# The last group's output products by half, and the third group's output projection at the end of the list

## The chip, the cores and the metric

The kernel runs on one core of a Trainium2 chip. The metric is the device time of one launch in microseconds (us). The five engines of the core have their own instruction streams: TensorE (PE, with its weight loads PEld), VectorE (DVE), ScalarE (ACT), GpSimd (POOL) and SyncE (SP), which issues most of the DMA. They wait for each other by semaphores only.

## The reference

One inference step of a trunk with two layers. 128 prompt tokens and 512 sample tokens, 640 in all, each a row of D = 1024 numbers in f32. Each layer is

```
h = rms_norm(x, g) * (1 + scale) + shift        # scale, shift, gate from SiLU(cond)
x = x + gate * branch(h)
```

Layer 0's branch is a Conformer convolution. Layer 1's branch, the one that the change touches, is a Mamba-2 scan in both directions:

```
u = h @ w_in                                    # z, x, b, c and the time steps
x, b, c = silu(depthwise_conv(x b c))           # 5 taps
y = scan forwards + scan backwards + d_skip * x # chunks of 128 tokens, 4 groups of 512 channels
y = rms_norm per group(y * silu(z)) @ w_out
```

Each scan works by chunks: within a chunk a 128x128 product of c and b, masked by decays, times x; between chunks a state that is carried on. A last RMSNorm of x with its gain gives the two outputs y; the scan's final states are outputs too.

## The kernel before

All matrix products are made in three: a number is split into a rounded part (hi) and the rest (lo), and a product is hi·hi + lo·hi + hi·lo. So 12 products of 128x512 stand for one output half chunk (128 tokens, 512 of the 1024 columns): four pieces of the 512 channels of a group, three products each.

Layer 1 is cut in tiles. The list `PLAN1` gives their order: `x`, `b`, `c`, `z` with a group and a number are projections of h (each 48 products of 128x320, line L1301), and `o` with a group and a half is the output projection of a finished group for one half of the columns (`out2`, 5 chunks of 12 products of 128x512, L1552). The generator `filler` takes them one by one. Group 3's output projection is not in the list: `last_products` makes it (L1907), chunk by chunk in the order `LAST` (4, 3, 0, 2, 1).

Beside the tiles runs the scan of each group (`group`): pcb (c times b, L1743), pst (a chunk's state, L1632), py (the masked product times x, L1763), po (the state's part, L1695) and pty (a transpose, L1722) on TensorE. On DVE stand the mask and decays (gf, L1571 and L1754), the state (stn, L1660), the state's part of y (yo, L1699), the transposed sum (xt, L1726), the multiplication by silu(z) (zs, L1781), the squares for the group's norm (ysq, L1827 and L1828), and the split of y in hi and lo (yl, L1810 or L1807). TensorE sums the squares (ssp, L1833). A drained product is scaled and gated by DVE (tmp, L1527, for the last group L1918) and added to x (L1531, L1921) by DVE or POOL. The convolution of the projections is on DVE too (L1345).

Nothing sets the order by hand. Each of these parts is a generator that yields operations with a guessed duration, keys it waits for and slots of rings of buffers it needs; the class `Order` keeps a clock for each engine and issues, again and again, the operation that can start first, with `PRIO1` deciding between equals. `run.lead` is the time that TensorE's operations are planned later than their inputs; it is 0.2 · (`PRIO1["lead"]` + 7), and 0.3 once `last_products` is through. So a new table gives another order of the same instructions. The real times are not those that the planner guessed: an engine works its list in order and waits where an input is late.

The last group's out weights, `w_out2[3, n]` for n = 0 to 3 (n = 0, 1 for half 0 of the columns, 2, 3 for half 1), come in four loads of 512 KB. Three go through the weight chain `w_chain` (buffers wf, wh, wl, DVE L1261), one is loaded late by `out_weights` into buffers that h leaves free after the last z tile (ACT L1874, DVE L1875). `last_products` waits for all four.

When both halves of a chunk have been added to x, with the sum of squares taken by ACT (L1922) as each half is done, DVE and ACT make the root of the mean square (`final`, L1929 to L1931), and `final_half` scales x (half 0 on ACT, L1945, after POOL has multiplied the gain, L1938; half 1 on DVE, L1947) and stores it (L1949).

## Time and profile before

| | us |
|---|---|
| median of 3 runs | 1062.21 (1061.73 to 1062.59) |
| profiled execution | 1061.69 |
| its span | 1059.8 |
| outside the span | 1.9 |
| PE busy | 1031.0 (97%) |
| DVE busy | 827.0 (78%) |
| ACT busy | 667.0 (63%) |
| POOL busy | 440.0 (42%) |
| first product of z32 | at 962.2 |
| end of z33, the last tile of the list | at 1002.5 |
| last product ends | at 1051.6 |

Times at the left of a row are microseconds from the start of the span. In rows of the timeline and of groups a line L12 is line 12 of the kernel, and `out<-in` names what is written and read. What stands in brackets at the end of a timeline row is how long the engine stood idle before it, and what ended that. A matmul on TensorE is pipelined: its length in a row is longer than the distance to the next one.

### The profile page before, as it was taken

How to read it: one execution, taken by the hardware profiler on the slowest of the kernel's cores; microseconds unless marked ns; L12 is line 12 of the kernel's file. 1: busy time of each engine (PE TensorE's matmuls, PEld its weight loads, DVE VectorE, ACT ScalarE, POOL GpSimd, SP SyncE). 2: the span in 40 equal slices, each digit the busy share in tenths (PEclk: the TensorE clock that was granted, in tenths of full speed). 3: DMA queues.
4: the chain of work that ended last, by engine and by line, in shares of the span. 5: the costliest groups of instructions: out<-in, count | busy, mean ns of one | idle time of the engine just before them, and what ended most of it. 6: DMA issues, size and time to landing. Idle time of an engine off the chain costs nothing.

```text
span 1059.8 us, 19157 instructions
## 1 busy us (share of the span) xinstructions
PE 1031.0 (97%) x7473; PEld 946.4 (89%) x7473; DVE 827.0 (78%) x1240; ACT 667.0 (63%) x1112; POOL 440.0 (42%) x443
## 2 busy tenths in 40 slices
PE   6999999999999999999999999999999999999986
PEld 3899999999999999999999988897879888998665
DVE  2599999998997689102678879789888687787897
ACT  6468788788687678433577666676556444572564
POOL 0029989978596511111000055335522544003642
PEclk9999999999999999999999999999999999999989
DMA  9598888788756667776212443434324344125413
GB/s 360 197 255 205 191 212 202 178 211 218 180 134 138 130 144 154 143 165 148 61 62 85 115 136 88 121 107 129 104 80 136 100 130 140 60 80 149 140 41 100
DMA packets 64362, 151.82 MB, mean 143 GB/s; under 512 B 9472, under 2 KB 22416, under 8 KB 64272
## 3 DMA queue, kind: packets, MB, share of 16 engines
q1 hardware_dynamic: 52480, 118.35, 36.0%
q0 software_dynamic: 8640, 30.94, 17.2%
q10 hardware_dynamic: 3152, 1.31, 0.5%
q8 instruction: 59, 0.97, 0.4%
q14 instruction: 31, 0.25, 0.1%
HBM read 145.45 MB, written 5.12 MB: 142 GB/s over the span
## 4 chain that ended last, share of the span: by engine, by line
PE 88%; DVE 5%; ACT 2%; DMA 2%; issue 2%; SPq 0%; POOL 0%; DVEq 0%; ACTq 0%; POOLq 0%
PE pz L1301 9%; PE xs L1301 8%; PE o L1552 8%; PE B L1301 2%; PE C L1301 2%; PE po L1695 2%; PE pst L1632 2%; PE o L1907 2%; PE py L1763 2%; PE o__4958 L157 1%; PE o__5267 L157 1%; PE o__5258 L157 1%; PE o__5245 L157 1%; PE o__4948 L157 1%; PE o__5238 L157 1%
## 5 line engine op out<-in xcount | busy, mean ns | idle before, releaser
L809 DVE SCALAR_TENSOR_TENSOR cva<-v,cst,cva 128x550 f32<-128x550 f32 (+12 forms) x346 | 270.2, 823 | 11.4 <-ACT cva L801 6.4
L881 POOL TENSOR_TENSOR cv<-cv,tp 128x490 f32<-128x490 f32 (+5 forms) x134 | 172.6, 1288 | 8.5
L840 ACT ACTIVATE tp<-v,cst 128x490 f32<-128x490 f32 (+5 forms) x134 | 92.4, 718 | 36.2 <-POOL cv L881 35.9
L424 ACT CAST wh<-wf 128x1024 fp32r<-128x1024 f32 x63 | 65.9, 1047 | 63.4 <-PE o__5267 L157 29.8
L1301 PE MATMUL pz<-h_hi,wh 128*128 128x320 f32 x256 | 86.3, 337 | 1.7 <-ACT up L1332 1.7
L1701 POOL TENSOR_TENSOR y<-y,yo 128x512 f32<-128x512 f32 x32 | 49.8, 1555 | 85.1 <-DVE yo L1699 81.5
L1301 PE MATMUL pz<-h_hi,wl 128*128 128x320 f32 x256 | 79.1, 309 | 0.0
L1301 PE MATMUL pz<-h_lo,wh 128*128 128x320 f32 x256 | 79.0, 309 | 0.0
L1301 PE MATMUL xs<-h_hi,wh 128*128 128x320 f32 x224 | 76.4, 341 | 0.0
L1345 DVE SCALAR_TENSOR_TENSOR xs<-up,cst,xs 128x642 f32<-128x642 f32 x64 | 66.3, 1037 | 10.2 <-ACT xs L1343 8.8
L1575 ACT ACTIVATE gf<-gf,cols 128x128 f32<-128x128 f32 x160 | 50.8, 391 | 29.8 <-DVE gf L1571 29.7
L1301 PE MATMUL xs<-h_hi,wl 128*128 128x320 f32 x224 | 69.3, 309 | 0.0
L1301 PE MATMUL xs<-h_lo,wh 128*128 128x320 f32 x224 | 69.1, 308 | 0.0
L1258 DVE TENSOR_TENSOR wl<-wf,wh 128x1024 fp32r<-128x1024 f32 x38 | 50.9, 1346 | 15.2 <-ACT wh L1249 15.2
L434 ACT ACTIVATE wl<-wh 128x1024 fp32r<-128x1024 f32 x58 | 61.6, 1061 | 1.7
L1569 POOL TENSOR_TENSOR gb<-gb,cols 128x512 f32<-128x512 f32 x20 | 25.1, 1255 | 85.6 <-DVE xs L1345 66.4
L435 POOL DMA_DIRECT2D wl<-w_in x43 | 37.4, 870 | 54.8 <-ACT wl L434 54.2
L1552 PE MATMUL o<-wh,yh 128*128 128x512 f32 x120 | 53.2, 443 | 0.0
L1301 PEld LDWEIGHTS pz<-h_hi,wh 128*128 128x128 f32 x256 | 48.1, 188 | 5.6 <-issue 3.4
L1249 ACT CAST wh<-wf 128x1024 fp32r<-128x1024 f32 x38 | 39.5, 1046 | 18.5 <-DMA wf<-w_xbc 6.1
L1301 PEld LDWEIGHTS pz<-h_lo,wh 128*128 128x128 f32 x256 | 48.2, 188 | 3.1 <-issue 2.9
L435 POOL DMA_DIRECT2D wl<-w_out x15 | 13.0, 865 | 90.4 <-ACT wl L434 90.4
(846 smaller groups left out, 3497.0 us busy)
## 6 DMA issues: line engine op xcount, KB each, us to landing
wf<-w_in SPq DMA_DIRECT2D x48, 512.0 KB, 3.7
wl<-w_in POOLq DMA_DIRECT2D x43, 512.0 KB, 6.6
wa<-w_ada SPq DMA_DIRECT2D x64, 256.0 KB, 5.8
wf<-w_out SPq DMA_DIRECT2D x32, 512.0 KB, 3.6
wf<-w_xbc SPq DMA_DIRECT2D x24, 512.0 KB, 3.6
gf<-acf SPq DMA_DIRECT2D x40, 256.0 KB, 4.2
wa<-w_ada SPq DMA_DIRECT2D x16, 512.0 KB, 10.6
wf<-w_z SPq DMA_DIRECT2D x16, 512.0 KB, 3.8
```

The costliest lines, as they stand in the source:

```text
L157: T.matmul(ps[:, b, at : at + t1 - t0], lhsT=w, rhs=h[:, t0:t1], start=first and n == 0, stop=last and n == 2)
L424: t = yield op(ACT, 1.05, lambda: S.copy(out=wh, in_=wf))
L434: yield op(ACT, 1.06, lambda: S.activation(out=wl, in_=wh.bitcast(F32), func=AF.Copy, scale=-1.0))
L435: t = yield op(PD, 0.7, lambda: G.dma_start(out=wl, in_=src, accum_op=ALU.add))
L809: t = yield op(VE, 0.24 + 0.01 * (hi - lo), lambda: V.scalar_tensor_tensor(out=rows64(accs[i], lo, hi), in0=rows64(vs[i], lo + d, hi + d), ...
L840: t = yield op(ACT, 0.72, lambda: S.activation(out=tp[:, :, 0 : hi - lo], in_=rows64(vs[i], lo + d, hi + d), func=AF.Copy, scale=w_dw(i, t ...
L881: t = yield op(PO, 1.3 + 0.019 * (hi - lo - 49), lambda: G.tensor_add(out=rows64(cv[i], lo, hi), in0=rows64(cv[i], lo, hi), in1=sgs["tp", ...
L1258: e_.tensor_sub(out=cell["wl"], in0=cell["wf"], in1=cell["wh"].bitcast(F32))
L1301: T.matmul(ps[:, b, at_ : at_ + t1 - t0], lhsT=w_, rhs=t_[:, t0:t1], start=k == 0 and n == 0, stop=k == nk - 1 and n == 2)
L1345: t = yield op(VL, 0.97, lambda: V.scalar_tensor_tensor(out=acc, in0=u[:, d : d + PW], scalar=c("w_c", j * 5 + d), in1=acc, op0=ALU.mult, ...
L1552: T.matmul(ps, lhsT=t_, rhs=w_, start=k == 0 and n == 0, stop=k == 3 and n == 2)
L1575: t = yield op(ACT, 0.39, lambda: S.activation(out=gv[:, h_, :], in_=gv[:, h_, :], func=AF.Exp, bias=cols1[ch][:, o8 + h_ : o8 + h_ + 1]), ...
```

## The change

There are four parts.

1. The tables `PRIO1`, `PLAN1` and `RB1` are others. In the list, z33 was the last tile, and half 1 of group 2's output projection (o21) stood ahead of it; now o21 is the last one, behind z33, and z30 and x32 have moved too. The planned lead of TensorE goes from 1.0 to 0.6. The ring xs gets 3 buffers instead of 2, st 6 instead of 7.
2. Of the last group's out weights two pieces come through the weight chain instead of three, and two are loaded late into the freed h buffers instead of one (`late_weights`, ACT L1878, DVE L1879). The late ones are those of half 1.
3. `last_products` is one generator for each chunk and half (L1910) and waits for the weights of its half only; halves of different chunks can change places. The lead of 0.3 is set when the first of them is through.
4. The last half chunk (chunk 1, half 1) is made in two pieces of 256 columns: 24 products of 128x256, two tmp (L1925), two additions to x (L1933), two squares (L1936), and one more addition of sums (L1946).

The diff, with its long tables cut:

```diff
-PRIO1 = {"lead": -2, ... "last_products": 3, "last_residual": 7, ... }
+PRIO1 = {"late_weights": -7, "lead": -4, ... "last_products": 5, "last_residual": -2, ... }
...
-PLAN1 = "z00 b0 c0 z01 x02 x03 x13 b1 x10 x12 x22 x11 z02 x20 c1 x23 z03 b2 z10 x21 o00 z11 x33 o01 z12 z13 z20 c2 z30 x30 z21 x32 o10 z22 c3 z23 z31 o11 b3 x31 o20 z32 o21 z33"
-RB1 = {"xs": 2, "st": 7, "gf": 2, "gb": 1}
+PLAN1 = "x02 z00 x03 b0 c0 z01 x10 x23 x20 z02 x12 z03 x13 x11 x21 b1 c1 c2 z10 x22 z11 o00 z12 b2 z13 o01 c3 z20 x31 o10 z21 x33 x30 z22 z23 o11 b3 z30 x32 z31 o20 z32 z33 o21"
+RB1 = {"xs": 3, "st": 6, "gf": 2, "gb": 1}
...
 
         def out_weights():
             yield key(("z", 3, 3))
-            for n in range(3):
-                yield key(("w", len(items) - 3 + n))
-                wh, wl = W[len(items) - 3 + n]
+            for n in range(2):
+                yield key(("w", len(items) - 2 + n))
+                wh, wl = W[len(items) - 2 + n]
                 for k in range(2):
-                    w3[n // 2, n % 2 * 2 + k] = wh[:, k * 512 : k * 512 + 512], wl[:, k * 512 : k * 512 + 512]
+                    w3[0, n * 2 + k] = wh[:, k * 512 : k * 512 + 512], wl[:, k * 512 : k * 512 + 512]
                 post(("w3", n), 0.0)
-            cell = {}
-
-            def load():
-                cell["wf"] = gp.tile([P, 1024], F32, tag="wf", bufs=2, name="wf")
-                nc.sync.dma_start(out=cell["wf"], in_=a["w_out2"][3, 3])
-            yield get("wf")
-            yield op(SP, 0.35, load, 1.35)
-            for k in range(2):
-                wh, wl = hbuf("wh3")[:, 0:512], hbuf("wl3")[:, 0:512]
-                wf, sn = cell["wf"][:, k * 512 : k * 512 + 512], c("sn_g", 14 + k)
-                yield op(ACT, 0.62, lambda: S.activation(out=wh, in_=wf, func=AF.Copy, scale=sn))
-                t = yield op(VL, 0.68, lambda: V.scalar_tensor_tensor(out=wl, in0=wf, scalar=sn, in1=wh.bitcast(F32), op0=ALU.mult, op1=ALU.subtract))
-                w3[1, 2 + k] = wh, wl
-            put("wf", t)
-            post(("w3", 3), t)
+
+        def late_weights():
+            yield key(("z", 3, 3))
+            for n in range(2):
+                cell = {}
+
+                def load():
+                    cell["wf"] = gp.tile([P, 1024], F32, tag="wf", bufs=2, name="wf")
+                    nc.sync.dma_start(out=cell["wf"], in_=a["w_out2"][3, 2 + n])
+                yield get("wf")
+                yield op(SP, 0.35, load, 1.35)
+                for k in range(2):
+                    wh, wl = hbuf("wh3")[:, 0:512], hbuf("wl3")[:, 0:512]
+                    wf, sn = cell["wf"][:, k * 512 : k * 512 + 512], c("sn_g", 12 + 2 * n + k)
+                    yield op(ACT, 0.62, lambda: S.activation(out=wh, in_=wf, func=AF.Copy, scale=sn))
+                    t = yield op(VL, 0.72, lambda: V.scalar_tensor_tensor(out=wl, in0=wf, scalar=sn, in1=wh.bitcast(F32), op0=ALU.mult, op1=ALU.subtract))
+                    w3[1, 2 * n + k] = wh, wl
+                put("wf", t)
+                post(("w3", 2 + n), t)
 
         LAST = ORDER[3]
 
-        def last_products():
-            for ch in LAST:
-                yield key(("split", 3, ch), *[("w3", n) for n in range(4)])
-                yh, yl = grp[3]["yh"], grp[3]["yl"]
-                for hf in range(2):
-                    yield get("mm")
-                    ps = mm("o2")[:, 0]
-                    for k in range(4):
-                        def step():
-                            wh, wl = w3[hf, k]
-                            hi, lo = tokens(yh, k, ch), yl[k][:, ch * 128 : ch * 128 + 128]
-                            for n, (t_, w_) in enumerate(((hi, wh), (lo, wh), (hi, wl))):
-                                T.matmul(ps, lhsT=t_, rhs=w_, start=k == 0 and n == 0, stop=k == 3 and n == 2)
-                        t = yield op(PE, 0.69, step)
-                    start(last_residual(ch, hf, ps), t)
+        def last_products(ch, hf):
+            yield key(("split", 3, ch), ("w3", 2 * hf), ("w3", 2 * hf + 1))
+            yh, yl = grp[3]["yh"], grp[3]["yl"]
+            for n, (c0, c1) in enumerate(pieces(ch, hf)):
+                yield get("mm")
+                ps = mm("o2")[:, 0, 0 : c1 - c0]
+                for k in range(4):
+                    def step():
+                        wh, wl = (w_[:, c0:c1] for w_ in w3[hf, k])
+                        hi, lo = tokens(yh, k, ch), yl[k][:, ch * 128 : ch * 128 + 128]
+                        for n, (t_, w_) in enumerate(((hi, wh), (lo, wh), (hi, wl))):
+                            T.matmul(ps, lhsT=t_, rhs=w_, start=k == 0 and n == 0, stop=k == 3 and n == 2)
+                    t = yield op(PE, 0.69 if c1 - c0 == 512 else 0.36, step)
+                start(last_residual(ch, hf, ps, n, c0, c1), t)
             run.lead = 0.3
 
-        fin = lp.tile([P, 5, 4], F32, name="fin")
-
-        def last_residual(ch, hf, ps):
+        def pieces(ch, hf):
+            return ((0, 256), (256, 512)) if (ch, hf) == (LAST[-1], 1) else ((0, 512),)
+
+        fin = lp.tile([P, 5, 5], F32, name="fin")
+
+        def last_residual(ch, hf, ps, n, c0, c1):
             yield key(("rs", 3, ch), ("gt", 3), ("res", ch, hf, 2))
             yield get("yo")
-            tmp = lp.tile([P, 512], F32, tag="yo", bufs=2, name="tmp")
-            t = yield op(VE, 0.75, lambda: V.scalar_tensor_tensor(out=tmp, in0=ps, scalar=grp[3]["rs"][:, ch : ch + 1], in1=gate_of(3, hf, ch), op0=ALU.mult, op1=ALU.mult))
+            tmp = lp.tile([P, 512], F32, tag="yo", bufs=2, name="tmp")[:, 0 : c1 - c0]
+            half = c1 - c0 < 512
+            t = yield op(VE, 0.45 if half else 0.75, lambda: V.scalar_tensor_tensor(out=tmp, in0=ps, scalar=grp[3]["rs"][:, ch : ch + 1], in1=gate_of(3, hf, ch)[:, c0:c1], op0=ALU.mult, op1=ALU.mult))
             put("mm", t)
-            x_ = xv(ch, hf)
-            t = yield either((VL, 0.66, lambda: V.tensor_add(out=x_, in0=x_, in1=as_part(tmp, ch))), (PO, 1.29, lambda: G.tensor_add(out=x_, in0=x_, in1=as_part(tmp, ch))), bias=0.2)
-            t = yield op(ACT, 0.62, lambda: S.activation(out=as_part(tmp, ch), in_=x_, func=AF.Square, accum_out=fin[:, ch, hf : hf + 1]))
+            x_ = xs_[:, 4 * hf + c0 // 128 : 4 * hf + c1 // 128, :]
+            x_ = part(x_, ch)
+
+            def as_x(z_):
+                return z_.rearrange("p (j n) -> p j n", n=128) if half else as_part(z_, ch)
+            if half:
+                t = yield op(VL, 0.42, lambda: V.tensor_add(out=x_, in0=x_, in1=as_x(tmp)))
+            else:
+                t = yield either((VL, 0.66, lambda: V.tensor_add(out=x_, in0=x_, in1=as_x(tmp))), (PO, 1.29, lambda: G.tensor_add(out=x_, in0=x_, in1=as_x(tmp))), bias=0.2)
+            t = yield op(ACT, 0.4 if half else 0.62, lambda: S.activation(out=as_x(tmp), in_=x_, func=AF.Square, accum_out=fin[:, ch, hf + n : hf + n + 1]))
             put("yo", t)
-            post(("fin", ch, hf), t)
+            post(("fin", ch, hf, n), t)
 
         def final(ch):
-            yield key(("fin", ch, 0), ("fin", ch, 1), ("fgb",))
-            r = fin[:, ch, 2:3]
+            r = fin[:, ch, 3:4]
+            yield key(("fin", ch, 0, 0), ("fin", ch, 1, 0), ("fgb",))
             yield op(VE, 0.15, lambda: V.tensor_add(out=r, in0=fin[:, ch, 0:1], in1=fin[:, ch, 1:2]))
+            if len(pieces(ch, 1)) > 1:
+                yield key(("fin", ch, 1, 1))
+                yield op(VE, 0.15, lambda: V.tensor_add(out=r, in0=r, in1=fin[:, ch, 2:3]))
             yield op(ACT, 0.24, lambda: S.activation(out=r, in_=r, func=AF.Sqrt, scale=1.0 / 1024, bias=epsb), "sqrt")
-            t = yield op(VE, 0.14, lambda: V.reciprocal(out=fin[:, ch, 3:4], in_=r))
+            t = yield op(VE, 0.14, lambda: V.reciprocal(out=fin[:, ch, 4:5], in_=r))
             start(final_half(ch, 0), t, "final")
             start(final_half(ch, 1), t, "final")
...
-            start(last_products(), 0.0)
+            start(late_weights(), 0.0)
+            for ch in LAST:
+                for hf in range(2):
+                    start(last_products(ch, hf), 0.0)
```

`final` waits for both pieces of the last half chunk and adds the second sum (L1946); its root and reciprocal are L1947 and L1948, `final_half` is L1962 on ACT and L1964 on DVE, `gained_half` L1955. The number of instructions stays the same on ACT; TensorE has 12 products more, DVE and POOL differ by a few.

How the order moves is shown at three places. The first is the end of z33. TensorE, before: the rows are what follows the last products of z33 (the scan of group 3) up to the first product of `last_products`.

```order
L1763 MATMUL py<-gf,xt 64x128 x8
L1695 MATMUL po<-stn,C 128x512
L1743 MATMUL pcb<-C,B 128x128
L1722 MATMUL pty<-cst,y 128x128 x4
L1833 MATMUL ssp<-ones,ysq 128x1
L1722 MATMUL pty<-cst,y 128x128 x4
L1763 MATMUL py<-gf,xt 64x128 x8
L1695 MATMUL po<-stn,C 128x512
L1743 MATMUL pcb<-C,B 128x128
L1907 MATMUL o_10997<-wh,yh 128x512
```

And after, at the same stage of the scan (py, ssp, pcb, pst, pty of group 3):

```order
L1552 MATMUL o_10799<-wl,yh 128x512
L1763 MATMUL py<-gf,xt 64x128 x8
L1833 MATMUL ssp<-ones,ysq 128x1
L1743 MATMUL pcb<-C,B 128x128
L1552 MATMUL o_10850<-wh,yh 128x512
L1552 MATMUL o_10850<-wh,yl 128x512
L1552 MATMUL o_10850<-wl,yh 128x512
L1632 MATMUL pst<-xw,Bt 128x512
L1722 MATMUL pty<-cst,y 128x128 x4
L1552 MATMUL o_10850<-wh,yh 128x512
L1552 MATMUL o_10850<-wh,yl 128x512
```

The scan's pieces stood in one block behind z33; now products of o21 (L1552, o_10799, o_10850) stand between them. DVE at the same place, before, from the second late weight (wl_10980) to the first chunk's drain (o_10997 is the first tile of `last_products`) and on:

```order
L1875 SCALAR_TENSOR_TENSOR wl_10980<-wf,cst,wh_10979 128x512
L1571 COPY_PREDICATED gf<-msk,gb 64x8x64
L1827 TENSOR_TENSOR ysq<-ysq 128x256
L1828 TENSOR_TENSOR ysq<-ysq 128x128
L1810 TENSOR_TENSOR yl<-zs,yh 128x128 x4
L1699 TENSOR_TENSOR yo<-po,cols_6274 128x512
L1571 COPY_PREDICATED gf<-msk,gb 64x8x64
L1747 SCALAR_TENSOR_TENSOR pcb,cbd<-pcb,cst 128x128
L1843 RECIPROCAL rs<-ss 128x1
L1918 SCALAR_TENSOR_TENSOR tmp<-o_10997,rs,gt 128x512
```

And after, from the third late weight (wl_10921) to the drain of o21's last chunk (o_10955):

```order
L1879 SCALAR_TENSOR_TENSOR wl_10921<-wf,cst,wh_10920 128x512
L1843 RECIPROCAL rs<-ss 128x1
L1527 SCALAR_TENSOR_TENSOR tmp<-o_10912,rs,gt 128x512
L1531 TENSOR_TENSOR x<-x,tmp 128x4x128
L1879 SCALAR_TENSOR_TENSOR wl_10969<-wf,cst,wh_10968 128x512
L1726 TENSOR_TENSOR xt<-xt,pty 128x512
L1571 COPY_PREDICATED gf<-msk,gb 64x8x64
L1781 TENSOR_TENSOR zs<-zs,xt 128x4x128
L1747 SCALAR_TENSOR_TENSOR pcb,cbd<-pcb,cst 128x128
L1749 SCALAR_TENSOR_TENSOR co<-cols_6275,cbd,cst 128x8
L1699 TENSOR_TENSOR yo<-po,cols_6274 128x512
L1527 SCALAR_TENSOR_TENSOR tmp<-o_10955,rs,gt 128x512
```

The late weights stood ahead of every drain of the last products; now there are four of them, and they stand between the drains (L1527, L1531) of o21's chunks.

The second place is DVE ahead of the first pair of gf (L1754) of group 2. Before (wl, L1258, is the lo part of projection weights; C and xs, L1345, are convolutions):

```order
L1345 SCALAR_TENSOR_TENSOR C<-up_6268,cst,C 128x642 x3
L1660 TENSOR_TENSOR stn<-stn,pst 128x512
L1345 SCALAR_TENSOR_TENSOR C<-up_6268,cst,C 128x642
L1258 TENSOR_TENSOR wl<-wf,wh 128x1024
L1660 TENSOR_TENSOR stn<-stn,pst 128x512
L1747 SCALAR_TENSOR_TENSOR pcb,cbd<-pcb,cst 128x128
L1749 SCALAR_TENSOR_TENSOR co<-cols_6275,cbd,cst 128x8
L1754 TENSOR_TENSOR gf<-gf,pcb 128x512 x2
```

And after:

```order
L1345 SCALAR_TENSOR_TENSOR xs<-up_6268,cst,xs 128x642 x2
L1850 RECIPROCAL rs<-ss 128x5
L1527 SCALAR_TENSOR_TENSOR tmp<-o_9241,rs,gt 128x512
L1531 TENSOR_TENSOR x<-x,tmp 128x4x128
L1345 SCALAR_TENSOR_TENSOR xs<-up_6268,cst,xs 128x642 x2
L1747 SCALAR_TENSOR_TENSOR pcb,cbd<-pcb,cst 128x128
L1527 SCALAR_TENSOR_TENSOR tmp<-o_9272,rs,gt 128x512
L1531 TENSOR_TENSOR x<-x,tmp 128x4x128
L1749 SCALAR_TENSOR_TENSOR co<-cols_6275,cbd,cst 128x8
L1754 TENSOR_TENSOR gf<-gf,pcb 128x512 x2
```

Drains of o10 (L1527, L1531) and convolutions of an x tile (xs, L1345) have come in ahead of that pair of gf; the states (stn) have gone behind it.

The third place is DVE's end of the program. Before (o_11287 is the last half chunk, L1947 the multiplication of a finished half):

```order
L1947 SCALAR_TENSOR_TENSOR x<-x,fin,fgb 128x4x128
L1918 SCALAR_TENSOR_TENSOR tmp<-o_11287,rs,gt 128x512
L1921 TENSOR_TENSOR x<-x,tmp 128x4x128
L1929 TENSOR_TENSOR fin<-fin 128x1
L1931 RECIPROCAL fin<-fin 128x1
L1947 SCALAR_TENSOR_TENSOR x<-x,fin,fgb 128x4x128
```

And after (o_11272 and o_11308 are the two pieces of the last half chunk, L1964 the multiplication):

```order
L1935 TENSOR_TENSOR x<-x,tmp 128x4x128
L1948 RECIPROCAL fin<-fin 128x1
L1925 SCALAR_TENSOR_TENSOR tmp<-o_11272,rs,gt 128x256
L1933 TENSOR_TENSOR x<-x,tmp 128x2x128
L1964 SCALAR_TENSOR_TENSOR x<-x,fin,fgb 128x4x128
L1925 SCALAR_TENSOR_TENSOR tmp<-o_11308,rs,gt 128x256
L1943 TENSOR_TENSOR fin<-fin 128x1
L1933 TENSOR_TENSOR x<-x,tmp 128x2x128
L1946 TENSOR_TENSOR fin<-fin 128x1
L1948 RECIPROCAL fin<-fin 128x1
L1964 SCALAR_TENSOR_TENSOR x<-x,fin,fgb 128x4x128
```

The last drain was one tmp and one x of 512 columns behind the multiplication of the chunk before; now there are two of each at 256 columns, and that multiplication stands between them.

More of the change, by code (lines that the diff above doesn't have):

```diff
@@ L1935, in gained_half @@
         def gained_half(ch, hf):
-            yield key(("fin", ch, hf), ("fgb",))
+            yield key(*[("fin", ch, hf, n) for n in range(len(pieces(ch, hf)))], ("fgb",))
             x_ = xv(ch, hf)
@@ L1941, in final_half @@
         def final_half(ch, hf):
-            x_, r = xv(ch, hf), fin[:, ch, 3:4]
+            x_, r = xv(ch, hf), fin[:, ch, 4:5]
             if hf == 0:
@@ L1961, in trunk @@
         n_items = len(items)
-        for n in range(3):
-            items.append((None, a["w_out2"][3, n], 12 + n % 2 * 2))
+        for n in range(2):
+            items.append((None, a["w_out2"][3, n], 12 + n * 2))
         def filler():
```

2 lines of the change are left out of this document (1 added, 1 removed).

## The prediction

> **What bounds the kernel now.** I read the page first, then busy time by stage, then TensorE's timeline and its waits. The page's part 4 (the chain that ended last) names TensorE for most of the span.
>
> ```profile
> PE 88%; DVE 5%; ACT 2%; DMA 2%; issue 2%; SPq 0%; POOL 0%; DVEq 0%; ACTq 0%; POOLq 0%
> ```
>
> So time is lost where TensorE stands. The windows view (length, then busy time with instructions of PE, PEld, DVE, ACT, POOL, then the granted clock, DMA share, GB/s) of the end of layer 1 shows where: 962.2 is the first product of z32, 1002.5 the end of z33, 1051.6 the last product, and 974.3 to 1027.9 runs from group 3's first py to its last.
>
> ```profile
> 962.20:1002.50 40.30, 40.19 (x218) 31.40 (x217) 32.18 (x46) 12.69 (x26) 23.27 (x19) 1.00 0.51 145
> 1002.50:1019.00 16.50, 11.53 (x58) 7.41 (x59) 15.62 (x34) 10.55 (x20) 6.30 (x6) 0.79 0.43 128
> 1019.00:1037.40 18.40, 18.06 (x92) 13.50 (x90) 16.98 (x38) 11.33 (x26) 11.86 (x8) 1.00 0.05 15
> 974.30:1027.90 53.60, 48.52 (x236) 34.97 (x238) 46.99 (x84) 27.47 (x56) 30.37 (x25) 0.94 0.41 113
> ```
>
> Before 1002.5 TensorE is full and DVE (VectorE) idles 40.30 − 32.18 = 8.1 us. Right after it the roles turn: DVE is busy 15.62 of 16.50 and TensorE 11.53. TensorE's timeline there (start, length, instruction, idle before it and its releaser):
>
> ```profile
> 1002.62 1.12 PE L1632 MATMUL pst<-xw,Bt 128*128 128x512 f32 x2 [0.23 <-POOL xw L1627]
> 1005.10 0.66 PE L1763 MATMUL py<-gf,xt 128*64 128x128 f32 x8 [0.60 <-DVE gf L1754]
> 1007.48 0.66 PE L1722 MATMUL pty<-cst,y 128*128 128x128 f32 x4 [0.45 <-ACT xt L1733]
> 1010.21 0.35 PE L1833 MATMUL ssp<-ones,ysq 128*128 128x1 f32 x2 [2.08 <-DVE ysq L1828]
> 1012.70 1.97 PE L1763 MATMUL py<-gf,xt 128*64 128x128 f32 x16 [1.63 <-issue]
> ```
>
> The idle pieces add up to 0.23 + 0.60 + 0.45 + 2.08 + 1.63 = 4.99 us. They fall where the last scan chunks of group 3 stand bare: nothing of z is left and the last products cannot start yet. Behind them the clock is halved:
>
> ```profile
> 1008.00:1012.00 4.00, 0.98 (x8) 0.64 (x6) 3.83 (x12) 3.62 (x6) 1.50 (x1) 1.00 0.69 192
> 1012.00:1018.00 6.00, 5.30 (x23) 3.78 (x24) 5.97 (x12) 1.73 (x3) 2.04 (x2) 0.50 0.02 4
> 727.00:730.00 3.00, 2.85 (x21) 2.87 (x22) 3.00 (x8) 2.22 (x4) 0.98 (x1) 1.00 0.00 0
> ```
>
> Six microseconds at 0.50 are 3.0 us of work lost, so the hole is 4.99 + 3.0 = 8.0 us. But in those six DVE is busy 5.97: the slow clock cost little that DVE would not have cost. Elsewhere in layer 1 TensorE stands seldom; the waits view (total, times, longest), of 540 to 680 and of 680 to 1060, has
>
> ```profile
> PE pz L1301 <- ACT up L1332: 1.7, 1, 1.7
> ...
> PE ssp L1833 <- DVE ysq L1828: 3.7, 2, 2.1
> PE ssp L1833 <- DVE ss L1837: 0.4, 1, 0.4
> PE pty L1722 <- POOL y L1701: 0.3, 1, 0.3
> ```
>
> 3.7 less the 2.08 above leaves 1.6, so the middle holds 1.7 + 1.6 + 0.4 + 0.3 = 4.0 us.
>
> **The change, part by part.** Prices of TensorE come from the chain of waits (start, length, count) and, for a 128x512 product, from the first and last of six starts.
>
> ```profile
> 962.20 7.04 PE pz L1301 x48
> 970.86 0.86 PE pst L1632 x2
> 1050.09 0.39 PE L1907 MATMUL o<-wh,yh 128*128 128x512 f32 x1
> ...
> 1051.22 0.39 PE L1907 MATMUL o<-wl,yh 128*128 128x512 f32 x1
> ```
>
> A 320-column product takes 7.04 / 48 = 0.147 us, a 512-column one (1051.22 − 1050.09) / 5 = 0.226, a pst (and a po, which has its shape) 0.86. DVE's prices are group means of 640 to 1060 (count, busy, mean ns, idle before):
>
> ```profile
> L1345 DVE SCALAR_TENSOR_TENSOR xs<-up,cst,xs 128x642 f32<-128x642 f32 x38 | 40.5, 1067 | 5.6 <-ACT xs L1343 4.9
> L1258 DVE TENSOR_TENSOR wl<-wf,wh 128x1024 fp32r<-128x1024 f32 x25 | 33.3, 1337 | 9.2 <-ACT wh L1249 9.2
> L1571 DVE COPY_PREDICATED gf<-msk,gb 64x512 f32<-64x512 int32 x36 | 31.6, 879 | 3.0 <-POOL gb L1569 2.5
> L1261 DVE SCALAR_TENSOR_TENSOR wl<-wf,cst,wh 128x512 fp32r<-128x512 f32 x30 | 26.6, 922 | 4.3 <-ACT wh L1252 4.3
> L1531 DVE TENSOR_TENSOR x<-x,tmp 128x512 f32<-128x512 f32 x30 | 25.4, 847 | 1.0
> L1527 DVE SCALAR_TENSOR_TENSOR tmp<-o,rs,gt 128x512 f32<-128x512 f32 x30 | 22.4, 746 | 11.0 <-PE o L1552 11.0
> L1699 DVE TENSOR_TENSOR yo<-po,cols 128x512 f32<-128x512 f32 x31 | 21.2, 684 | 6.9 <-PE po L1695 6.8
> L1781 DVE TENSOR_TENSOR zs<-zs,xt 128x512 f32<-128x512 f32 x20 | 13.5, 713 | 1.6 <-ACT zs L1422 0.8 <-ACT zs L1423 0.7
> L1807 DVE TENSOR_TENSOR yl<-zs,yh 128x512 fp32r<-128x512 f32 x15 | 11.4, 794 | 0.0
> L1828 DVE TENSOR_TENSOR ysq<-ysq 128x128 f32<-128x128 f32 x20 | 10.9, 543 | 0.7
> L1827 DVE TENSOR_TENSOR ysq<-ysq 128x256 f32<-128x256 f32 x20 | 10.6, 532 | 3.5 <-ACT ysq L1823 3.2
> L1875 DVE SCALAR_TENSOR_TENSOR wl<-wf,cst,wh 128x512 fp32r<-128x512 f32 x2 | 2.4, 1179 | 0.0
> ```
>
> *o21 behind z33, last products per half.* Between group 3's first and last py TensorE gets 45 products of 320 columns, 36 of 512 (9 of o, 27 last ones), a po and some 0.6 us of transposes and sums more than before: 6.6 + 8.1 + 0.9 + 0.6 = 16.2 us. DVE gets there two L1261 (1.84), four drains of products (one L1527, three L1925, 0.746 each: 2.98) with their x additions (0.847 each: 3.39), two yo (1.37), xt, zs, a yl, a pair of ysq and a reciprocal (2.9), and two late weights (2.36): 14.8 us. Before, the stretch took 53.60 us, with DVE busy 46.99 and idle 6.6. If DVE idles just as long after, the stretch takes 53.6 + 14.8 = 68.4 us for 53.6 + 16.2 = 69.8 us of the old progress: a gain of 1.4. If DVE never idles it takes 46.99 + 14.8 = 61.8, a gain of 8.0. These are the bounds. I take 3.0, near the lower one, because DVE's idle time lies in z32 and z33, whose products give it little, and both still stand together, now both ahead of o21. The cover that o21 gives is counted within; without it the 8.0 us hole stays. One wait is new there: a last product takes a PSUM slot that the tmp of the product two before it frees. The third one (o_11075) so waits for tmp<-o_10989, ahead of which DVE has two L1261, an L1571 and a yo, 1.84 + 0.88 + 0.68 = 3.4 us, while TensorE has a po and twelve products, 0.86 + 2.7 = 3.6: hidden by 0.2, and if DVE is later, all last products stand behind it.
>
> *Late weights.* One more 512 KB load, with two ACT and two DVE instructions, goes from the weight chain into the late place; loads and instructions in all stay the same, so SP's queue and ACT carry no more. They must land before the first last product, which is now a half that needs them. DVE's fourth late weight stands ahead of the drain of o21's last chunk, so the last 12 products of o21 (2.7 us) and a po hide it; uncovered it would cost the two late weights and the drain pair between them, 2 × 1.18 + 0.75 + 0.85 = 4.0 us. The range holds that. I take nothing.
>
> *Last half chunk in two pieces.* 24 products of 256 columns for 12 of 512. A line through 0.147 and 0.226 gives an estimate of 0.121 at 256, so +0.2 us; were the time per column unchanged it would be 0. No row has that shape. At the end the chain (start, length) is
>
> ```profile
> 1051.65 0.76 DVE tmp L1918
> 1052.43 0.72 DVE x L1921
> 1053.17 0.73 ACT tmp L1922 x2
> ```
>
> and each of the three shrinks to about 0.45 (128x256 stands at 0.53 in L1827, with POOL beside it), so −0.9. Against it, DVE now has the multiply of the chunk before (L1964, about 0.75) and a small add ahead of the last piece: its first piece is done 1.4 us before the end, its drain pair needs 0.9, so the multiply ends some 0.3 us late, and the adds take 0.15. Net −0.9 + 0.2 + 0.3 + 0.15 ≈ −0.3, between −0.9 and +0.5.
>
> *New tables.* They reorder all of layer 1; counts on each engine stay. TensorE's planned lead falls from 1.0 to 0.6 us, that is 0.4 less slack for each dependence. The worst place I find is from group 1's last py to group 2's first: TensorE has 144 products of 320 and 51 of 512 columns plus 4.1 us of small ones, 21.1 + 11.5 + 4.1 = 36.7. DVE has twelve L1345 (eight of 1.067, four of C at most that: 12.8), three L1258 (4.0), four each of L1571, L1261, L1531, L1527 (13.6), five L1807 (4.0), five pairs of ysq (5.4), and 6.6 of smaller ones: 46.4, so 9.7 more than TensorE. Before, DVE had less than TensorE there (about 40 against 46, by the same prices), with no products of o there. DVE is ahead of TensorE when that place starts, by how much no row shows. So the middle lies between −4.0 (its waits gone) and +9.7; I take +0.5, since these long means include POOL's presence and waits in the middle stayed at 1.7 or less each.
>
> **The sum.** 1061.69 (the profiled execution) − 3.0 − 0.3 + 0.5 = 1058.9. It lies 0.52 under the median of 1062.21, so I forecast **1059.4**.
>
> The Trainium skill (TensorE: Matmul & The Clock Gate, section "What's actually happening") says that TensorE is halved after an idle window of about 3.4 us and freed after a busy one of that length. This trace agrees: 0.50 behind four microseconds with 0.98 us of work, 1.00 behind the gap of 1.57 us in 727 to 730. By that rule the 3.0 us would come off on top, and the sum would be 1056.4; it is rival D below.
>
> **The rivals.** *A, DVE never idles in the stage:* gain 8.0, middle unchanged: 1062.21 − 8.0 − 0.3 = 1053.9. For it: TensorE has o21 at every gap. Against: DVE's 8.1 us idle ahead of 1002.5. Chance 0.11. *D, the half clock goes and with it 3.0 us more:* if no 4 us with under 1 us of work remain, 1059.4 − 3.0 = 1056.4. For it: o21's sixty products lie between the scan's pieces; against: DVE busy 5.97 of 6.00 under the slow clock. Chance 0.11. *B, DVE sets the pace and idles as before:* gain 1.4, so 1062.21 − 1.4 − 0.3 + 0.5 = 1061.0. For it: DVE 15.62 of 16.50 in the hole. Against: o21's drains can fill some of the idle time. Chance 0.13. *C, slower:* DVE arrives late at group 2's first py. If half of the 9.7 us excess is not covered, TensorE stands 4.8 us in one piece and loses 3.0 us to the clock as it did behind 1008: 1059.4 − 0.5 + 7.8 = 1066.7. It decides from a stall of 5.4 us on, clock included (1058.9 + 5.4 = 1064.3, 0.2% over before). For it: the sums; against: means with POOL's presence in them, and DVE's unknown advance. Chance 0.19. That the change does not do what it says is excluded by the order: o21 does stand behind z33.
>
> **How the numbers follow.** Forecast 0.46, with its own range 1057.5 to 1062. A measurement of this kernel can tell about 0.2%, 2.1 us, from no change: faster is under 1060.1, slower over 1064.3. Of the forecast's 0.46 I put 0.34 under 1060.1 and 0.12 over it. A and D are faster (0.22), B is the same (0.12, and 0.01 slower), C slower (0.17) or the same (0.02). That gives 0.56, 0.26 and 0.18. The range of 1054.5 to 1064.5 leaves out most of A (0.08) and somewhat over half of C (0.11).
>
> **What would show it.** Right: between z33's end and the last product TensorE's idle sum falls from 4.99 to 2 to 3 us, with o L1552 beside py and pty; DVE is busy over nine tenths of that stage; the last chain has tmp and x of about 0.45 us. A would show DVE without gaps from z32 on; B the same idle DVE under z32 and z33 and stalls on ysq or gf; C a gap of over 3 us at a py near group 2's start, with the clock at 0.5 behind it; D a stage at 1.00 throughout. I am wrong if the middle's idle sum moves by more than 2 us from its 4.0, or if o L1910's first products wait for wl.

## The result, and the profile after

| | before | changed |
|---|---|---|
| median | 1062.59 us (1061.73 to 1063.07, 5 runs) | 1071.36 us (1070.44 to 1074.11, 5 runs) |
| ratio | | 1.009, 95% interval 1.0076 to 1.0105 |
| profiled execution's span | 1059.8 | 1069.6 |
| first product of layer 1 starts | 545.65 | 547.71 |
| from there to the first product of z32 ("middle") | 416.38 | 423.58 |
| from there to the last product's end ("stage") | 89.58 | 88.89 |
| from the last product's end to the end of the last scaling ("tail") | 3.82 | 4.64 |
| from there to the end of the span | 4.42 | 4.76 |

The change made the kernel 0.9% slower; 1059.4 was forecast, with a range up to 1064.5. The rows of the table add up to the difference of the spans: 2.1 of start, 7.2 of middle, −0.7 of stage, 0.8 of tail, 0.3 of stores, 9.7 us in all. The start is not the change's, as the last section shows. So the place is the middle, for which the forecast had +0.5. (By the timeline z32 begins at 962.03 before; 962.2 is where the chain of waits first has it.)

The windows view puts the middle and the stage of both kernels side by side (length, then busy time of PE, PEld, DVE, ACT, POOL, clock, DMA share, GB/s). Before:

```profile
545.65:962.03 416.38, 414.08 (x2637) 368.69 (x2638) 344.01 (x483) 257.41 (x477) 129.97 (x100) 1.00 0.36 108
962.03:1051.61 89.58, 84.09 (x429) 63.89 (x427) 78.53 (x144) 42.63 (x92) 44.91 (x36) 0.96 0.38 106
```

After:

```profile
547.71:971.29 423.58, 416.76 (x2640) 368.68 (x2641) 343.14 (x490) 257.07 (x475) 130.99 (x103) 1.00 0.36 107
971.29:1060.18 88.89, 82.54 (x439) 62.26 (x437) 79.90 (x143) 43.16 (x93) 37.27 (x31) 1.00 0.36 103
```

No engine got more work in the middle: DVE (VectorE) 344.01 and 343.14, ACT 257.4 and 257.1, POOL 130.0 and 131.0. DVE has some 80 us of idle time there. TensorE's idle time grew from 416.38 − 414.08 = 2.3 to 423.58 − 416.76 = 6.8 us, and its busy time by 2.7 for the same products; a later run shows that most of these 2.7 are waits too (a wait shorter than the modelled tail of the product before it is not counted as idle). The waits view of the changed kernel's middle (total, times, longest):

```profile
PE po L1695 <- DVE stn L1660: 1.7, 2, 0.9
PE o L1552 <- DVE tmp L1527: 1.4, 1, 1.4
PE ssp L1833 <- DVE ysq L1828: 1.2, 4, 0.5
PE pty L1722 <- DVE stn L1660: 0.9, 1, 0.9
PE ssp L1833 <- DVE co L1749: 0.7, 1, 0.7
PE pty L1722 <- POOL y L1701: 0.5, 1, 0.5
PE pst L1632 <- POOL xw L1627: 0.3, 1, 0.3
```

There is no single hole. Eleven short waits stand there, nine of them for DVE. The kernel before had three (in brackets):

```profile
690.45 0.66 PE L1722 MATMUL pty<-cst,y 128*128 128x128 f32 x4 [0.29 <-POOL y L1701]
713.19 0.35 PE L1833 MATMUL ssp<-ones,ysq 128*128 128x1 f32 x2 [0.43 <-DVE ss L1837]
727.15 0.35 PE L1833 MATMUL ssp<-ones,ysq 128*128 128x1 f32 x2 [1.57 <-DVE ysq L1828]
```

In both kernels a further wait of 1.7 us stands just ahead of the middle and ends with its first product. How one of the eleven comes about is seen at 862.74, on TensorE and then on DVE's timeline:

```profile
858.66 1.02 PE L1632 MATMUL pst<-xw,Bt 128*128 128x512 f32 x2
862.74 1.12 PE L1695 MATMUL po<-stn,C 128*128 128x512 f32 x2 [0.87 <-DVE stn L1660]
```

```profile
857.46 1.51 DVE L1531 TENSOR_TENSOR x<-x,tmp 128x512 f32<-128x512 f32 x1
858.89 3.20 DVE L1258 TENSOR_TENSOR wl<-wf,wh 128x1024 fp32r<-128x1024 f32 x2
862.01 0.68 DVE L1660 TENSOR_TENSOR stn<-stn,pst 128x512 f32<-128x512 f32 x1
```

pst is done within a microsecond of 858.66, but DVE first makes two splits of projection weights (3.20 us together), and only then adds pst to the state for which po waits. The planner had put them in this order by its own durations.

The hole of the kernel before lay in the stage. The waits view of its TensorE, after:

```profile
PE ssp L1833 <- DVE ysq L1828: 2.4, 2, 1.4
PE py L1763 <- DVE gf L1754: 1.2, 1, 1.2
PE po L1695 <- DVE stn L1660: 1.2, 1, 1.2
PE o L1910 <- DVE tmp L1925: 0.7, 2, 0.4
PE o L1552 <- ACT zs L1423: 0.6, 1, 0.6
```

6.1 us of waits stand there, against 5.4 before, but none over 1.4, and the clock is 1.00 for the whole stage. The 3.0 us that the half clock had cost are won, and the stage is still only 0.7 us shorter. From the end of z33 (1002.5 before, 995.99 after) to the last product DVE has next to no idle time, 46.35 of 49.10 us busy before and 62.11 of 64.19 after:

```profile
1002.50:1051.60 49.10, 43.72 (x210) 32.32 (x210) 46.35 (x99) 29.77 (x67) 21.47 (x17) 0.93 0.27 75
995.99:1060.18 64.19, 59.14 (x294) 43.63 (x293) 62.11 (x121) 34.90 (x76) 24.87 (x20) 1.00 0.28 81
```

So DVE's own work is the likely bound of that stretch. No run shortened more than one of its operations there, so this is not shown. The tail, on DVE and on POOL:

```profile
1060.02 1.82 DVE L1964 SCALAR_TENSOR_TENSOR x<-x,fin,fgb 128x512 f32<-128x512 f32 x1
1061.75 0.47 DVE L1925 SCALAR_TENSOR_TENSOR tmp<-o,rs,gt 128x256 f32<-128x256 f32 x1
```

```profile
1060.02 1.27 POOL L1955 TENSOR_TENSOR x<-x,fgb 128x512 f32<-128x512 f32 x1 [2.84 <-ACT tmp L1936]
```

The multiplication of the chunk before (L1964) starts together with POOL's multiplication by the gain and takes 1.82 us; the last one of the program, with POOL idle, takes 0.75. So the last piece, whose products end at 1060.18, is drained from 1061.75 on.

### The profile page after: what moved, and what is told of

It is laid out like the page before. It is cut to its first block, busy times and chain, and to the rows that moved or that the text cites. A ratio compares the mean times of both kernels' runs of the same rounds, so it can differ in the third digit from the quotient of the medians.

```text
span 1069.6 us, 19147 instructions
## 1 busy us (share of the span) xinstructions
PE 1032.0 (96%) x7485; PEld 945.3 (88%) x7485; DVE 828.8 (77%) x1246; ACT 668.0 (62%) x1113; POOL 433.5 (41%) x442
## 5 line engine op out<-in xcount | busy, mean ns | idle before, releaser
L1701 POOL TENSOR_TENSOR y<-y,yo 128x512 f32<-128x512 f32 x32 | 44.5, 1389 | 87.4 <-DVE yo L1699 87.3
L1345 DVE SCALAR_TENSOR_TENSOR xs<-up,cst,xs 128x642 f32<-128x642 f32 x64 | 63.4, 993 | 11.3 <-ACT xs L1343 9.6
L1646 POOL TENSOR_TENSOR stn<-st_f,decb 128x512 f32<-128x512 f32 x4 | 4.2, 1057 | 157.1 <-DMA st_f<-st_f 157.1
L1258 DVE TENSOR_TENSOR wl<-wf,wh 128x1024 fp32r<-128x1024 f32 x38 | 49.5, 1312 | 7.9 <-ACT wh L1249 7.7
L1552 PE MATMUL o<-wh,yh 128*128 128x512 f32 x120 | 52.7, 439 | 2.0 <-DVE tmp L1527 1.4
```

Of the source, the lines that this page charges most:

```text
L1258: e_.tensor_sub(out=cell["wl"], in0=cell["wf"], in1=cell["wh"].bitcast(F32))
L1345: t = yield op(VL, 0.97, lambda: V.scalar_tensor_tensor(out=acc, in0=u[:, d : d + PW], scalar=c("w_c", j * 5 + d), in1=acc, op0=ALU.mult, ...
L1552: T.matmul(ps, lhsT=t_, rhs=w_, start=k == 0 and n == 0, stop=k == 3 and n == 2)
L1701: t = yield op(PO, 1.29, lambda: G.tensor_add(out=y, in0=y, in1=yo))
```

## The experiments

Each run was also timed against the kernel before on the same chip. Middle, stage and tail are as above, each read from one profiled execution.

| kernel | median us | ratio to before, 95% | middle | stage | tail |
|---|---|---|---|---|---|
| changed kernel | 1071.36 | 1.0076 to 1.0105 | 423.6 | 88.9 | 4.6 |
| old tables, new code | 1066.66 | 1.0027 to 1.0052 | 417.1 | 93.7 | 4.4 |
| new tables, old code | 1077.19 | 1.0123 to 1.0150 | 424.2 | 96.3 | 4.3 |
| changed, last half chunk in one piece | 1069.76 | 1.0045 to 1.0072 | 423.5 | 88.7 | 4.7 |
| changed, old lead | 1077.67 | 1.0133 to 1.0163 | 429.2 | 90.5 | 4.6 |
| old tables with o21 last, new code | 1066.88 | 1.0014 to 1.0046 | 416.5 | 93.5 | 4.7 |
| old tables with o21 last, old code | 1067.12 | 1.0023 to 1.0051 | 416.4 | 92.1 | 3.8 |
| changed, short taps | 1065.44 | 1.0013 to 1.0036 | 419.0 | 88.3 | 4.6 |
| before, short taps | 1061.02 | 0.9972 to 0.9994 | 415.6 | 89.0 | 3.8 |
| old tables, new code, one late weight | 1062.33 | 0.9986 to 1.0005 | 416.3 | 89.9 | 3.8 |
| before, lead 0.6 | 1076.56 | 1.0118 to 1.0144 | 425.7 | 93.4 | 3.8 |
| changed, short weight splits | 1066.12 | 1.0015 to 1.0043 | 419.6 | 89.5 | 4.6 |
| changed, both short | 1063.14 | 0.9998 to 1.0018 | 416.6 | 88.8 | 4.6 |
| changed, old list of tiles | 1088.44 | 1.0219 to 1.0273 | 436.4 | 94.0 | 3.4 |
| changed, old priorities and lead | 1068.13 | 1.0042 to 1.0087 | 422.0 | 89.0 | 3.9 |
| before, lead 1.2 | 1073.58 | 1.0087 to 1.0121 | 428.3 | 89.3 | 3.8 |

### Tables or code

```diff
 # in the changed kernel
-PRIO1, PLAN1, RB1 of the change
+PRIO1, PLAN1, RB1 of the kernel before, "late_weights": -5
```

> The changed code (two late weights, products per chunk and half, last half chunk in two pieces) with the three tables of the kernel before; the order in the middle of layer 1 is then nearly that of the kernel before. Theory T (the loss comes from the order that the new tables make in the middle, +7 us there by the traces): within 2 us of the kernel before, 1061 to 1065, with the middle's TensorE idle sum back at about 2 us. Rival C (the loss comes from the new code at the end, four late weights on DVE and halves out of order): 1067 or more.

```diff
 # in the kernel before
-PRIO1, PLAN1, RB1
+PRIO1, PLAN1, RB1 of the change
```

> The code of the kernel before with the three new tables. Theory T: 1069 to 1073, as slow as the changed kernel, with z32 starting some 7 us later after layer 1's start than in the kernel before (423 to 424 us instead of 416.4). Rival C: 1061 to 1065.

The middle follows the tables in both runs: 417.1 with the old ones, 424.2 with the new ones. That part of the theory holds. The times do not: 1066.66 and 1077.19 both lie above what was expected. Each half of the change alone is slower than the kernel before, by 0.4% and 1.4%, and the two together by 0.9%. The stage is what differs: 93.7 and 96.3 us where either half is missing, 88.9 with both. With the old tables and the new code, TensorE waits in that stage almost only for the squares:

```profile
PE ssp L1833 <- DVE ysq L1828: 6.7, 4, 2.3
```

### The late weights alone

```diff
 # old tables, new code, and the weights as in the kernel before
-            for n in range(2):     # two pieces through the chain, two late
+            for n in range(3):     # three pieces through the chain, one late
```

> The tables of the kernel before and the changed code without its late weights: three pieces of the last out weights through the chain and one late, as before; last products per chunk and half, last half chunk in two pieces. With both late pieces (run with the old tables) the stage from z32 to the last product took 93.7 us against 89.6. Theory W (the fourth late weight on DVE, ahead of the scan's last chunks, is what that cost): stage 86 to 90, time 1060 to 1063. Rival H (products per half, let in early, put the drains ahead of the scan's operations on DVE): stage 91 to 94, time 1065 to 1068.

Theory W holds. Without the second late piece the stage falls from 93.7 to 89.9 us and the time from 1066.66 to 1062.33, so with the old tables the second late piece, two more late splits (L1879) on DVE, costs 4.3 us. Part of that is the clock: the traces have it at half speed for 6.8 us of the stage with the second late piece and for 3.4 us without, which is 1.7 us of work. Products per half and the last half chunk in two pieces, which are still in this kernel, make no difference to before (ratio 0.9986 to 1.0005). Its tail of 3.84 against 3.82 says the same of the two pieces.

### o21 behind z33 alone

```diff
-PLAN1 = "... o20 z32 o21 z33"
+PLAN1 = "... o20 z32 z33 o21"
```

> The tables of the kernel before, with one edit in the list of tiles: o21 behind z33; the changed code. The middle of layer 1 then stays nearly as before (416 to 418 us). Theory O (o21 behind z33 fills the hole, as forecast: 3 us off the stage from z32 to the last product): stage 86 to 88, time 1059 to 1063. Rival (DVE is the bound of that stage, and the order that follows leaves its idle time where it was): stage 89 to 94, time 1063 to 1067.

> The kernel before with one edit in the list of tiles: o21 behind z33; its code unchanged (one late weight, products chunk by chunk, last half chunk in one piece). Theory O (o21 alone fills the hole): 1057 to 1061. Rival (without the split by halves the last products wait longer, as in the run of the new tables with the old code, whose stage took 96 us): 1064 to 1070.

Both rivals give the right times: the stage grows to 92.1 us with the old code (from 89.6), and stays at 93.5 with the new (from 93.7). The reason of the first fits too: DVE's idle time in the stage is 14.2 us, and was 14.1. The reason of the second does not: with the old code the last products wait for nothing. There the hole did not close, it moved. TensorE with the old code:

```profile
1003.97 1.10 PE L1695 MATMUL po<-stn,C 128*128 128x512 f32 x2
1010.95 1.97 PE L1763 MATMUL py<-gf,xt 128*64 128x128 f32 x16 [5.87 <-issue]
```

DVE meanwhile:

```profile
1005.71 1.41 DVE L1261 SCALAR_TENSOR_TENSOR wl<-wf,cst,wh 128x512 fp32r<-128x512 f32 x2
1007.04 0.68 DVE L1699 TENSOR_TENSOR yo<-po,cols 128x512 f32<-128x512 f32 x1
...
1007.71 0.73 DVE L1261 SCALAR_TENSOR_TENSOR wl<-wf,cst,wh 128x512 fp32r<-128x512 f32 x1
...
1008.57 1.54 DVE L1261 SCALAR_TENSOR_TENSOR wl<-wf,cst,wh 128x512 fp32r<-128x512 f32 x1
...
1010.17 1.27 DVE L1754 TENSOR_TENSOR gf<-gf,pcb 128x512 f32<-128x512 f32 x2
```

The profile names no releaser for the 5.87 us, but py starts when the first of the two gf is done. o21's weights were in use until 1003. They hold two of the three slots of the weight chain until then, so the last group's weights come later and their four splits (L1261) stand ahead of the gf that py waits for. That the slots made them late is read from the code and from this order; no run changed the number of slots.

### The last half chunk

```diff
-            return ((0, 256), (256, 512)) if (ch, hf) == (LAST[-1], 1) else ((0, 512),)
+            return ((0, 512),)
```

> The changed kernel with the last half chunk in one piece of 512 columns; nothing else moves. The trace of the changed kernel has 4.64 us from the last product's end to the last multiplication's end, the kernel before 3.82. Theory P (two pieces cost, since DVE multiplies the chunk before ahead of the last piece while POOL multiplies too, 1.82 us instead of 0.75): 0.5 to 1.0 us faster than the changed kernel, 1070.4 to 1070.9. Rival (two pieces save what three shorter operations save): 0.3 to 0.9 slower than it.

The time is 1069.76 against 1071.36, on the side of theory P, though by more than it said; the intervals of the two against before (1.0045 to 1.0072 and 1.0076 to 1.0105) barely part. The traces show the tails alike, 4.64 and 4.69, and, counted from layer 1's first product, the last scaling ends 0.25 us earlier in one piece. So two pieces save nothing here. That they cost 1.6 us is not shown. Nor is the reason of theory P the whole of it: in one piece the multiplication of the chunk before does take 0.75 us, but it still makes the drain start 0.52 us behind the last product's end, and now the addition stands beside POOL's multiplication and takes 1.10 us instead of 0.69:

```profile
1060.92 1.10 DVE L1935 TENSOR_TENSOR x<-x,tmp 128x512 f32<-128x512 f32 x1
```

### The lead

```diff
 # in the changed kernel
-"lead": -4
+"lead": -2
```

> The changed kernel with the planned lead of TensorE back at 1.0 us instead of 0.6. Theory L (the loss is the smaller lead: DVE is late by less than 0.4 more than planned at most stalls): 1064 to 1067, TensorE's idle sum of layer 1 from 13 to about 8 us. Rival (the loss is the order of the tiles and priorities, DVE being late by more than any lead): another order, but 1069 to 1075.

```diff
 # in the kernel before
-"lead": -2
+"lead": -4
```

> The kernel before with the planned lead of TensorE at 0.6 us instead of 1.0, one entry of a table. Theory L (the smaller lead is what the middle lost): middle over 420 us, with short waits for DVE as in the changed kernel, time 1066 or more. Rival (the lead alone matters little; it is the place of the weight splits and tiles): middle 415 to 418, time 1060 to 1064.

```diff
 # in the kernel before
-"lead": -2
+"lead": -1
```

> The kernel before with the planned lead of TensorE at 1.2 us instead of 1.0. With 0.6 its middle took 425.7 instead of 416.4. Theory L (more lead, fewer waits): middle 414.5 to 416.5, time 1059 to 1063. Theory R (the new plan is another draw): middle 419 or more, time over 1065.

This one number moves the middle of the kernel before from 416.4 to 425.7 when it is smaller and to 428.3 when it is larger. Given back to the changed kernel, it makes the middle 5.6 us longer, and the time of 1077.67 lies above both expectations. So the expectation for the smaller lead in the kernel before came true, yet its reason did not: the lead has no direction. Each value gives another list for each engine.

### Is it DVE

The following kernels keep the order of the operations on all engines, and shorten operations of DVE only (what they leave out is in the expectations).

```diff
-V.scalar_tensor_tensor(out=acc, in0=u[:, d : d + PW], ..., in1=acc, ...)
+V.scalar_tensor_tensor(out=acc[:, 0:64], in0=u[:, d : d + 64], ..., in1=acc[:, 0:64], ...)
```

> The changed kernel with every tap of layer 1's convolution on DVE (L1345, 96 operations, 92 us) made on 64 of its 642 columns, so the convolution is left unfinished; TensorE's order and all other instructions are the same, and some 75 us of DVE work go. Theory D (the 7.2 us that the middle lost are DVE being late under the new order): the middle falls by 5 to 7 us, to 416 to 419 us, and its TensorE idle sum from 6.8 to under 2. Rival E (TensorE's own order, transfers or ACT cost them): the middle stays over 421.

> The kernel before with the same shortened taps (the convolution is left unfinished). Theory D: the middle falls only by the 2.3 us of idle time that it has, from 416.4 to 414 to 415 us, so the two middles come within 3 us of each other. Rival E: they stay 6 to 8 us apart.

The middle of the changed kernel falls by 4.6 us, to 419.0, that of the kernel before by 0.8; they come from 7.2 to 3.4 us apart. That is just outside what theory D said, and TensorE's idle sum is 4.1 us where it said under 2. Theory D has about half of the loss so far, and waits stayed. The one shown above is still there, with the two splits even longer:

```profile
853.27 4.04 DVE L1258 TENSOR_TENSOR wl<-wf,wh 128x1024 fp32r<-128x1024 f32 x2
857.23 0.67 DVE L1660 TENSOR_TENSOR stn<-stn,pst 128x512 f32<-128x512 f32 x1
```

```diff
-e_.tensor_sub(out=cell["wl"], in0=cell["wf"], in1=cell["wh"].bitcast(F32))
+e_.tensor_sub(out=cell["wl"][:, 0:128], in0=cell["wf"][:, 0:128], in1=cell["wh"][:, 0:128].bitcast(F32))
 # and in dense_steps
-wl[:, wofs[k] : wofs[k] + 128]
+wl[:, 0:128]
```

> The changed kernel with the lo part of the projection weights (L1258) made on 128 of its 1024 columns only, and the third product of each projection step reading these columns every time, so the projections are inexact; the order on TensorE and all counts are the same. About 45 us of DVE work go, at the places where weight splits stand ahead of the scan's operations. Theory S (splits standing ahead of stn and ysq make TensorE wait; the shortened taps left these waits as they were): the waits of po and pty for stn and of ssp for ysq in the middle go, middle 417 to 420 us. Rival (the splits wait for ACT or a load, and their length does not matter): middle 421 to 424, the waits for stn still 0.9 each.

> The changed kernel with both shortened taps and shortened weight splits (convolution unfinished, projections inexact), the order on TensorE the same: some 120 us of DVE work gone. If all that the middle lost is DVE being late, the middle comes to 415 to 417 us, the level of the kernel before; if a part is in TensorE's order, loads or ACT, it stays at 418 or more with waits that name these.

Shorter splits alone bring the middle to 419.6, and the wait of po for stn is gone. (In that trace the clock is 0.50 from 837.7 to 841.1, behind a wait of 2.09 us for tmp, which is 1.7 us of work in the 419.6.) Both together bring it to 416.6, which is the middle of the kernel before, with the changed kernel's own order on TensorE. The windows and waits of that run:

```profile
546.04:962.68 416.64, 414.33 (x2640) 368.68 (x2641) 251.75 (x489) 257.03 (x475) 120.63 (x103) 1.00 0.36 109
```

```profile
PE o L1552 <- DVE tmp L1527: 0.8, 1, 0.8
PE ssp L1833 <- DVE co L1749: 0.6, 1, 0.6
PE pty L1722 <- DVE stn L1660: 0.5, 1, 0.5
PE ssp L1833 <- DVE ysq L1828: 0.3, 1, 0.3
```

TensorE's busy time is back at 414.33, so 2.4 of the 2.7 us were waits. So 6.9 us of the middle go when DVE's operations are shorter, with 251.75 us of DVE work in it instead of 343.14. The kernel before was not run with both edits. It gained 0.8 us by the taps alone, and its waits in the middle are 2.3 us in all. If it can gain no more than these, what the changed kernel gains beyond it lies between 4.6 and 6.1 of the 7.2 us. That much is shown to be DVE being late under the new order; the rest is open. POOL's operations also became shorter without being edited (120.63 us instead of 130.99), and how much of the gain came by way of POOL was not separated. The stage, 88.8, did not gain; it holds no taps and one such split.

### Which table

```diff
 # in the changed kernel: only the list of tiles is old
-PLAN1 of the change
+PLAN1 of the kernel before
```

> The changed kernel with the old list of tiles; priorities, rings and code are the new ones. Theory R (any new plan of this kernel loses, since the planner's durations are guesses and only the old tables happen to fit the real ones): middle over 420, time 1066 or more. Theory N (the list of tiles is what makes DVE late): middle 415 to 418.5, as with the old tables.

```diff
 # in the changed kernel: only the priorities and the lead are old
-PRIO1 of the change
+PRIO1 of the kernel before, "late_weights": -5
```

> The changed kernel with the old priorities (and the old lead of 1.0 us); list of tiles, rings and code are the new ones. Theory R: middle over 420, time 1066 or more. Theory N: over 420 too. Theory Q (the priorities and the smaller lead make DVE late): middle 415 to 418.5.

Theory R gives the right numbers in both: the middle is 436.4 with the old list and the new priorities, 422.0 with the new list and the old priorities. So neither the new list nor the new priorities have to be there for a loss. The rings are the new ones in both runs (xs 3, st 6), and no run gave back the rings alone, so their part in the changed kernel's loss is open; the two other leads in the kernel before lost 9.3 and 11.9 us with the old rings. All six plans of the middle that were new in some entry (the new tables, two mixtures, three leads) took 422.0 to 436.4. The five kernels with DVE's full work and all the old entries ahead of the stage took 416.3 to 417.1; TensorE and DVE have the same order there in all five, so these are repeats of one plan and show how far a middle differs from execution to execution. (The three with the plan of the change and DVE's full work took 423.5 to 424.2.)

These runs do not show that it is DVE that makes the other five new plans slower. Each of them has the half clock in its middle, for 3.4 to 13.6 us (the changed kernel has none), and among their longest waits are some for ACT, such as 2.6 us for zs with the lead at 0.6.

## Why the prediction was wrong

**What bounds the kernel: right.** TensorE sets the time, and it loses where DVE is late.

**The new tables (+0.5 us, chosen between −4.0 and +9.7): wrong, and the step that failed.** The middle lost 7.2. The bounds held it; the choice did not. The sign that was written for being wrong came: counted as there, with the 1.7 us ahead of the first product, the middle's idle sum went from 4.0 to 8.5 us. The reason for the choice was that the waits of the kernel before were short and that group means are long. But those short waits belong to one order. The six new plans that were run lost 5.6 to 20.1 us in the middle against the old one. The sum looked for one worst place, by totals over some 36 us; what was lost was in eleven places, with totals unchanged. Those totals do not see the order: what counts is which operations stand between a product and the DVE operation that waits for it, as with the two splits ahead of stn.

**Rival C (1066.7): right on the side and the engine, wrong on the mechanism.** It put one gap of 4.8 us at group 2's first py, with a half clock behind it. That py, at 848, did not wait. Around it, from 816.7 to 862.7, stand four waits with 3.1 us together, of the 6.8 of the middle, and the clock stayed at 1.00. What it described did come a little ahead of that py, in the run with short splits: 2.09 us of wait and then the half clock.

**o21 behind z33 (−3.0 us, bounds 1.4 to 8.0 of gain): wrong.** The whole stage gained 0.7, and the move alone lost 2.5 us with the old tables and code. The step took DVE's work and TensorE's over the stretch and left out when each was to be had: in the run of the move alone o21 was spent before the scan's last chunks needed cover, and the last group's weights came late. In the changed kernel DVE's idle time in the stage did fall, from 11.1 to 9.0 us, but its work grew by 1.4 us and TensorE's waits are 6.1 us for 5.4. From z33's end to the last product TensorE's idle sum is 4.9 us, where 2 to 3 were forecast; that DVE would be busy over nine tenths there came true, at 97%.

**Late weights (0 us, or 4.0 if uncovered): not settled.** They cost 4.3 us with the old tables. There o21 does not stand behind z33, so the cover that the 0 rested on is not there, and the 4.3 is near the price for that case; but only a part is what the 4.0 was made of. In the trace the two late splits stand ahead of the scan's last pair of gf, which, counted from z32, is 2.7 us later than without them; the rest comes as a later wait for ysq and as half clock. That the two numbers agree is luck. With o21 last, the new code's stage is 1.4 us longer than the old code's (93.5 and 92.1), late weights and halves together. In the changed kernel itself the term was not measured alone.

**Two pieces (−0.3 us): wrong in one price, for a tail that grew by 0.8.** Products of 256 columns come 0.12 us apart in the tail's rows, close to the estimate of 0.121:

```profile
1058.73 0.28 PE L1910 MATMUL o<-wh,yl 128*128 128x256 f32 x1
1058.85 0.28 PE L1910 MATMUL o<-wl,yh 128*128 128x256 f32 x1
```

And tmp and x take 0.47 and 0.43, near the 0.45. The multiplication ahead of the last piece was put at 0.75; beside POOL it took 1.82. With the old tables and one late weight the two pieces have a tail of 3.84, as before, and in the changed kernel one piece has 4.69; so what lengthens the tail is how DVE's and POOL's operations fall together there, not the split. The Trainium skill says (SBUF — State Buffer, section "Who interferes with whom") that a DVE operation with two SBUF inputs contends with a GpSimd one that reads SBUF. The trace agrees, at 1.82 against 0.75.

**Rival D (the clock): its condition came true, its price did not.** The stage ran at 1.00 throughout and gained 0.7 us, not 6. This fits the reason for which the 3.0 us were not added, that DVE was busy 5.97 of those 6.00 us and a faster TensorE would wait for it; but the late weights and the order changed in the same stage, so it is not shown by itself.

**The range and chances.** 1054.5 to 1064.5 with 0.18 for slower treated the new plan as a small disturbance. Here it is the larger effect: the middle lost 7.2 us, the stage and the tail together 0.1.

## What to carry to other kernels

Where a list scheduler works with guessed durations, a new table can change the whole order, and the short waits of the old order are no measure of the new one's. Count what stands between a product and the operation that waits for it; totals over a stage do not show it. A single number of the table costs 9 to 12 us in the middle of this kernel in either direction, so a change of structure should be timed with the tables as they were, and with each of its parts alone.

To find out whether an engine's lateness is the cause, shorten its operations and keep every list as it is. Here that gave back 6.9 us where 7.2 had been lost, while five more orders only showed that other plans lose too. Make the same edit in the kernel before as well, since part of what comes back may be had there too.
